# Turned memory probabilities in the raw-weight ring, and queries leaving PSUM by one engine after the other

## The chip, the cores and the metric

The kernel runs on one core of a Trainium2 chip. A time is the device time of one execution in microseconds (us), from the first to the last instruction and what little lies around it. The core has five engines with a queue each: TensorE (PE in the profile; its weight loads are PEld), VectorE (DVE), ScalarE (ACT), GpSimd (POOL) and SyncE (SP), which here only issues transfers. Each engine takes its instructions strictly in the order in which the program gives them, and waits at the head of its queue for the semaphores that the instruction needs. Matrix products land in PSUM, which has eight banks of 512 float32 per partition; VectorE and ScalarE read them from there.

## The reference

One inference step of a two-layer trunk, for a prompt of 512 tokens and a sample of 32 tokens, 544 columns in all. Layer 0 mixes tokens with RWKV-7, layer 1 with differential attention. Each layer is an RMS norm, one input projection, the token mixer, a cross-attention of four heads over 256 memory tokens, a SiLU gate, an output projection and a residual. The change touches layer 1 only:

```python
q, k, v, qm, gate = jnp.split(h @ w_in, [MIX_W, 2 * MIX_W, 3 * MIX_W, 3 * MIX_W + MEM_W], axis=-1)
...
attn = probs(q1, k1) - lam * probs(q2, k2)                  # 12 heads, two score maps each
o = rmsnorm(einsum('bhqk,bkhd->bqhd', attn, v_all), subln) * (1.0 - lam_init)
...
s = jnp.einsum('bthd,bmhd->bhtm', q, mk) * MEM_HD ** -0.5   # 4 memory heads of 128, 256 memory tokens
p = jax.nn.softmax(s, axis=-1)
y_mem = jnp.einsum('bhtm,bmhd->bthd', p, mv)
```

Outputs are the two token streams, the RWKV states and the keys and values of attention and memory.

## The kernel before, in words

**Layout.** Activations lie transposed: 128 features on the partitions, 544 tokens along the free axis. A projection is done in blocks of 128 output columns. One block is 48 matmuls: two halves of 272 tokens (one PSUM bank each, from the pool `psg` of three banks), and per half 8 slices of the 1024 inputs times 3 products (high part of the weight by high and low part of the activation, low part by high part). The loop is `steps`, line 463; one turn of it issues one matmul and is called a step below.

**Layer 1** (`diff_layer`, line 1940) is one stream of 56 such blocks: for each of the 12 heads a value, a key and a query block, then the gate blocks, and for heads 1, 3, 5 and 7 also a memory-query block and its gate. Everything else (scores, softmax, turning, DMA) is a list of events `ev`, each with a step at which it is issued. `at(f + x, ...)` puts an event x steps behind the begin f of its head. So the order of all queues is written out by hand: `Queue` and `tie` (lines 127 to 155) chain every instruction of an engine behind the one before it.

**Weights.** Layer 1's input projection uses scaled float16 weights. Their raw float32 blocks lie in four buffers in the space of the old low part of the activations (`h16s` in the profile). ScalarE writes the high half (`whs`), GpSimd scales the raw block and subtracts to get the low half. The power-of-two scale of a block is made by VectorE (`scales`, line 347) at step 36 of a block, from a sum that TensorE puts into column 480 of the bank that the block's first half uses. The earlier ring `raw` (pool `wp`, five buffers of 128 x 512 float32, line 1935) holds raw float32 halves in layer 0 and again for the output projection of layer 1. `self.ahead` is the list of blocks that are still to be loaded; its last 16 are those of the output projection.

**Queries.** `make_q` (line 1975) writes `qp`, the query split into a high part and a remainder for two row halves of 64 (the two score maps). For each half of the tokens, `parts` runs four instructions on one PSUM bank: ScalarE copies rows 0 to 63, VectorE subtracts that copy from the same rows; then the same for rows 64 to 127. In the second token half a ScalarE copy of the 32 sample columns (`qs`) follows. The framework lets no two engines touch one PSUM bank at a time, so of two instructions on one bank on different engines the later one in the program waits for the earlier.

**Memory heads in layer 1.** `mem_steps` (line 1217) is a generator with its turns at the steps of `MEMAT1`. The normalised probabilities of five token tiles are turned by VectorE in three pieces (two of 128 x 512, one of 128 x 256), at steps 330, 402 and 420 behind the begin f of the head (330, 400 and 430 for head 7). Each piece goes through `spread` (line 1911): VectorE transposes 32 x 32 blocks into the tile `to`, then SP stores `to` to DRAM in four parts (one part for the short piece), and a later load brings the turned matrix back (`mpT`). `to` has one buffer, so a turn waits until the stores of the turn before have landed. `spread` is called 15 times: 3 turns for each of 4 memory heads, and one for the cached keys of each of 3 groups of heads (4 steps behind the begin of heads 1, 5 and 9).

**Scores.** For each head, four tiles of scores (`scores`, `powers`, `turned`): TensorE writes two maps into the pools `psx` (one bank) and `psc` (two banks), VectorE takes the peaks (`snm`), ScalarE the exponentials (`pt`, `ps_s`), and VectorE joins and turns them (`pk`). TensorE's next tile of scores needs the bank of `psx`, which ScalarE's first exponential frees.

**The end.** The output projection (`w_out`, line 1346) loads its weights through the `raw` ring, and SP's queue also carries 12 copies of keys and values from DRAM to DRAM (`kv_out`, line 2239).

Of the kernel before, what the change touches and what calls it, by code (L numbers as in the profile page):

```python
# [9 lines left out]
F32 = mybir.dt.float32  # L10
# [4 lines left out]
AF = mybir.ActivationFunctionType  # L15
ALU = mybir.AluOpType
AX = mybir.AxisListType

P = 128
# [43 lines left out]
RAWS = 5  # L63
# [71 lines left out]
class Trunk:  # L135
# [1775 lines left out]
    def spread(self, x, rows, scr=None, blocks=range(4)):  # L1911

        if scr is None:
            scr = self.dp.tile([rows, P], F32, tag="spread", name="spread", bufs=4)[:]
        to = self.stage.tile([P, 512], F32, tag="to", name="to", bufs=1)[:, :rows]
        self.ve.transpose(to, x)

        def store():
            for b in blocks:
                self.se.dma_start(scr.rearrange("(n r) q -> r n q", r=32)[:, :, 32 * b : 32 * b + 32],  # L1920
                                  to[32 * b : 32 * b + 32].rearrange("p (n c) -> p n c", c=32))
            return scr

        return store
# [15 lines left out]
    def diff_layer(self, dq, p, mp, mctx, pool_early, order, made):  # L1940
# [6 lines left out]
        rows = [slice(0, 64), slice(64, P)]  # L1947
# [28 lines left out]
        def make_q(st):  # L1976
            def make(w):
                st["qp"] = qp = dq.tile([P, 2, T], F32R, tag="qp", name="qp", bufs=QB)

                def parts(ps, c):  # L1980
                    for m in range(2):
                        hi, inv = qp[rows[m], m, c], w[2][rows[m]]
                        self.ae.activation(hi, ps[rows[m], :], AF.Copy, scale=inv)
                        self.ve.scalar_tensor_tensor(qp[rows[1 - m], m, c], ps[rows[m], :], inv, hi.bitcast(F32),
                                                       ALU.mult, ALU.subtract)
                    if c.start:
                        self.ae.activation(st["G"]["qs"][:, st["j"], :], ps[:, TH - TS :], AF.Copy, scale=w[2])
                yield from self.steps(w, parts)
            return make

# [259 lines left out]
        for h, st in enumerate(sts):  # L2250
# [24 lines left out]
            if h in MEM1:  # L2275
                m = MEM1.index(h)
# [144 lines left out]
```

## Time and profile before

| what | value |
|---|---|
| median of 3 runs | 1396.15 us (1393.91 to 1396.59) |
| the profiled execution | 1400.69 us, of which the span is 1398.9 us |
| TensorE busy | 1315.5 us, 94% of the span |
| VectorE, ScalarE, GpSimd busy | 66%, 62%, 45% |
| granted TensorE clock, mean over the span | 0.981 of full |
| layer 1's input projection and attention | about 843 to 1262 us from the span's start |

How to read the profile's rows: a row of a timeline has the start (us from the span's start), the duration of the merged instructions, the engine, the line, the operation, `out<-in` by tile names, the shapes, and in square brackets the idle time of the engine just before and what ended it. Nearly all rows have line 132, that of the helper `Queue` that issues everything; the tile names tell them apart. A matmul's duration includes its latency, so rows of matmuls overlap. SPq rows are the issuing of transfers by SyncE.

### The profile page before, as it was taken

What the parts mean: (1) busy time and instruction counts of PE and PEld (TensorE: products, weight loads), DVE (VectorE), ACT (ScalarE), POOL (GpSimd) and SP (SyncE); (2) the same over time, 40 slices, a digit from 0 to 9 for tenths busy, and PEclk for the clock granted to TensorE, in tenths of its full rate; (3) what the DMA queues carried; (4) which work ended last, traced back from release to release, by engine and by line L of the source; (5) the groups of instructions that cost most, each with busy time, mean ns of one, the idle gap of its engine ahead of it and who ended that gap; (6) DMA issues with size and microseconds to landing.
All of it is one profiled execution on the core that took longest, in us unless ns stands there. A gap on an engine that the chain in (4) does not pass through costs nothing. (4 is left out here: it accounts for less than half of the span.)

```text
span 1398.9 us, 32065 instructions
## 1 busy us (share of the span) xinstructions
PE 1315.5 (94%) x11713; PEld 1195.5 (85%) x11713; DVE 925.5 (66%) x2391; ACT 862.9 (62%) x2316; POOL 624.5 (45%) x1103
## 2 busy tenths in 40 slices
PE   6999999999999999899999999989999998999797
PEld 6998899999999998898899987868777776878797
DVE  7766777787778777765763455656785568666343
ACT  7665677767776777565553367757655775773221
POOL 2227576556755585520120066545554554561000
PEclk9999999999999999999999999999999999999898
DMA  7542223332233323234384456766776667666421
GB/s 238 177 138 66 60 55 90 84 76 71 70 85 76 81 63 79 73 88 126 91 266 134 122 147 162 156 149 157 171 165 145 151 140 178 140 156 206 136 69 64
DMA packets 418296, 171.53 MB, mean 123 GB/s; under 512 B 195209, under 2 KB 402578, under 8 KB 418138
## 3 DMA queue, kind: packets, MB, share of 16 engines
q1 hardware_dynamic: 417994, 168.96, 46.3%
q8 instruction: 92, 1.51, 0.5%
q14 instruction: 66, 0.54, 0.1%
q10 hardware_dynamic: 144, 0.52, 0.1%
HBM read 130.84 MB, written 41.92 MB: 123 GB/s over the span
## 5 line engine op out<-in xcount | busy, mean ns | idle before, releaser
L132 PE MATMUL ps_g<-h,whs 128*128 128x272 f16 x2688 | 339.8, 282 | 15.2 <-POOL whs L132 11.8
L132 PEld LDWEIGHTS <-whs 128*128 128x128 f16 x2688 | 256.2, 99 | 73.3 <-POOL whs L132 15.7
L132 PE MATMUL ps_g<-hl,whi 128*128 128x272 f32 x976 | 284.2, 297 | 0.6 <-POOL hl L583 0.5
L132 PE MATMUL ps_g<-hh,wlo 128*128 128x272 f32 x912 | 277.8, 305 | 1.2 <-DVE wlo L132 1.2
L132 PE MATMUL ps_g<-hh,whi 128*128 128x272 f32 x912 | 275.0, 302 | 0.6 <-ACT hh L132 0.6
L872 POOL TENSOR_TENSOR tm<-u,m 102x84 f32<-102x84 f32 (+23 forms) x372 | 156.0, 419 | 165.9 <-DMA m<-sc 137.9
L132 DVE TENSOR_TENSOR wlo<-raw,whi 128x512 fp32r<-128x512 f32 x208 | 150.0, 736 | 84.5 <-ACT whi L132 80.9
L132 PEld LDWEIGHTS ps_g<-hl,whi 128*128 128x128 f32 x976 | 183.9, 191 | 2.4 <-POOL hl L583 0.7
L132 ACT CAST whi<-raw 128x512 fp32r<-128x512 f32 x210 | 125.3, 616 | 97.4 <-PE ps_g L132 45.4
L132 PEld LDWEIGHTS ps_g<-hh,whi 128*128 128x128 f32 x912 | 174.8, 192 | 4.1 <-ACT hh L132 1.0
L132 PEld LDWEIGHTS ps_g<-hh,wlo 128*128 128x128 f32 x912 | 174.2, 191 | 4.6 <-DVE wlo L132 1.9
L874 POOL TENSOR_TENSOR u<-u,tm 102x84 f32<-102x84 f32 (+23 forms) x372 | 159.5, 429 | 29.1
L132 POOL TENSOR_SCALAR h16s<-h16s 128x512 f32<-128x512 f32 x112 | 79.1, 717 | 151.5 <-ACT whs L132 150.3
L132 PE MATMUL ps_g<-hi,whi 128*128 128x272 f32 x448 | 130.6, 292 | 10.2 <-ACT hi L132 10.2
L132 PE MATMUL ps_g<-lo,whi 128*128 128x272 f32 x448 | 130.9, 292 | 1.2 <-DVE lo L132 1.1
L132 PE MATMUL ps_g<-hi,wlo 128*128 128x272 f32 x448 | 130.4, 291 | 0.5 <-DVE wlo L132 0.5
L132 POOL TENSOR_TENSOR whs<-h16s,whs 128x512 f16<-128x512 f32 x112 | 128.2, 1165 | 0.2
L132 PEld LDWEIGHTS ps_g<-hi,whi 128*128 128x128 f32 x448 | 85.5, 191 | 10.5 <-ACT hi L132 10.4
L132 PEld LDWEIGHTS ps_g<-lo,whi 128*128 128x128 f32 x448 | 85.5, 191 | 2.3 <-DVE lo L132 2.3
L132 PEld LDWEIGHTS ps_g<-hi,wlo 128*128 128x128 f32 x448 | 85.6, 191 | 0.9 <-DVE wlo L132 0.9
L132 DVE SCALAR_TENSOR_TENSOR SB<-ps_c,dl,sd 64x64 f32<-64x64 f32 x168 | 47.4, 282 | 42.9 <-PE ps_c L132 38.8
L132 ACT ACTIVATE whs<-h16s 128x512 f16<-128x512 f32 x112 | 74.9, 715 | 0.9 <-PE ps_g L132 0.9
(419 smaller groups left out, 2840.5 us busy)
## 6 DMA issues: line engine op xcount, KB each, us to landing
raw<-in_rw_in_dram SPq DMA_DIRECT2D x114, 256.0 KB
h16s<-in_df_in_dram SPq DMA_DIRECT2D x112, 256.0 KB
raw<-in_w_out_dram SPq DMA_DIRECT2D x64, 256.0 KB
ptr<-pk SPq DMA_DIRECT2D x44, 160.0 KB
aT<-ptr SPq DMA_DIRECT2D x11, 640.0 KB
scr<-sg SPq DMA_DIRECT2D x96, 68.0 KB
out_dram<-scr SPq DMA_DIRECT2D x6, 1024.0 KB
m<-sc SPq DMA_DIRECT2D x36, 128.0 KB
```

Of the source, the lines that this page charges most:

```text
L132: return lambda *a, **k: self.trunk.tie(self, issue(*a, **k))
L872: nc.gpsimd.tensor_tensor(tm[:, :n, :wd], u3[:, :n, kx : kx + 1].to_broadcast(sh), m3[:, kx : kx + 1, kx + 1 :].to_broadcast(sh), ALU.mult)
L874: nc.gpsimd.tensor_tensor(u3[:, :n, kx + 1 :], u3[:, :n, kx + 1 :], tm[:, :n, :wd], ALU.add)
```

## The change

Two edits. In `spread`, while more than 17 blocks are still to be loaded, the tile `to` is taken from the five buffers of the ring `raw` instead of its own single buffer. In `make_q`, ScalarE's copies of both row halves (and `qs`) come before VectorE's two subtractions in the program. No instruction, shape or transfer is added or taken away, and the order on each single engine is as before.

```diff
         if scr is None:
             scr = self.dp.tile([rows, P], F32, tag="spread", name="spread", bufs=4)[:]
-        to = self.stage.tile([P, 512], F32, tag="to", name="to", bufs=1)[:, :rows]
+        if len(self.ahead) > 17:
+            to = self.wp.tile([P, 512], F32, tag="raw", name="to", bufs=RAWS)[:, :rows]
+        else:
+            to = self.stage.tile([P, 512], F32, tag="to", name="to", bufs=1)[:, :rows]
         self.ve.transpose(to, x)
...
                 def parts(ps, c):
                     for m in range(2):
-                        hi, inv = qp[rows[m], m, c], w[2][rows[m]]
-                        self.ae.activation(hi, ps[rows[m], :], AF.Copy, scale=inv)
-                        self.ve.scalar_tensor_tensor(qp[rows[1 - m], m, c], ps[rows[m], :], inv, hi.bitcast(F32),
-                                                       ALU.mult, ALU.subtract)
+                        self.ae.activation(qp[rows[m], m, c], ps[rows[m], :], AF.Copy, scale=w[2][rows[m]])
                     if c.start:
                         self.ae.activation(st["G"]["qs"][:, st["j"], :], ps[:, TH - TS :], AF.Copy, scale=w[2])
+                    for m in range(2):
+                        self.ve.scalar_tensor_tensor(qp[rows[1 - m], m, c], ps[rows[m], :], w[2][rows[m]],
+                                                       qp[rows[m], m, c].bitcast(F32), ALU.mult, ALU.subtract)
                 yield from self.steps(w, parts)
```

## The prediction, made before the changed kernel was run

> **What bounds the kernel now.** I read the busy time by stretches first, then who waits for whom inside the stretch that the change touches, then the timelines of four engines around the longest waits. Stretches (columns: length; busy us and count of PE, PEld, DVE, ACT, POOL; granted clock; DMA share; GB/s):
>
> ```profile
> core 0 of [0], span 1398.9 us
> 843.00:1262.00 419.00, 389.35 (x3307) 319.21 (x3305) 277.52 (x826) 282.24 (x765) 228.68 (x238) 0.98 0.68 155
> ```
>
> The change lies in these 419 us. TensorE is busy for 389.35 of them, VectorE and ScalarE for about two thirds. So TensorE sets the pace there, and only its 29.65 us without work, and its time at a lower clock, can be won. TensorE's waits inside the stretch, and in layer 1 VectorE's and ScalarE's waits on the edited places (total, times, longest):
>
> ```profile
> PE ps_g L132 <- POOL whs L132: 10.3, 10, 2.3
> PE ps_s L132 <- ACT pt L132: 8.7, 5, 2.5
> PE ps_g L132 <- DVE h16s L132: 3.2, 2, 1.7
> PE ps_s L132 <- DVE os L132: 2.3, 1, 2.3
> ...
> DVE to L132 <- DMA mspread<-to: 17.8, 4, 7.2
> ...
> ACT qp L132 <- DVE qp L132: 45.6, 24, 8.1
> ```
>
> VectorE stands 17.8 us in front of the single tile `to`, four times, once per memory head. ScalarE stands 45.6 us in the 24 evacuations of queries, at the second row half each time. Neither engine is the bound, so what counts is which of these waits reach TensorE. Place A, in time order per engine (SP; DVE; ACT; PE):
>
> ```profile
> 916.74 5.13 SPq L132 DMA_DIRECT2D mspread<-to  x5
> ...
> 912.39 0.49 DVE L132 SCALAR_TENSOR_TENSOR qp<-ps_g,h16s,qp 64x272 fp32r<-64x272 f32 x1 [2.47 <-ACT qp L132]
> 913.44 0.51 DVE L132 SCALAR_TENSOR_TENSOR qp<-ps_g,h16s,qp 64x272 fp32r<-64x272 f32 x1 [0.55 <-ACT qp L132]
> 921.10 0.45 DVE L132 STREAM_TRANSPOSE to<-mp 128x256 f32<-128x256 f32 x1 [7.16 <-DMA mspread<-to]
> ...
> 924.87 0.49 DVE L132 TENSOR_REDUCE snm<-ps_s 128x1 f32<-128x128 f32 x2
> ...
> 922.73 0.48 ACT L132 ACTIVATE qp<-ps_g,h16s 64x272 fp32r<-64x272 f32 x1 [8.07 <-DVE qp L132]
> ...
> 926.33 0.35 ACT L132 ACTIVATE pt<-ps_s,snm 128x128 f32<-128x128 f32 x1
> ...
> 921.79 2.49 PE L132 MATMUL ps_g<-h,whs 128*128 128x272 f16 x20 [1.68 <-DVE h16s L132]
> 926.82 0.58 PE L132 MATMUL ps_s<-kh,qp 128*128 128x256 f32 x1 [2.54 <-ACT pt L132]
> ```
>
> The third turn of the memory head (921.10) waits 7.16 us until the stores of the second have landed; SP gets to them only at 916.74. Behind it in VectorE's queue stand the scales of a weight block and the first subtraction of the second query half. TensorE waits 1.68 us for the scales (they read column 480 of a bank that it needs). ScalarE waits 8.07 us for the subtraction, so its exponentials start late, and TensorE waits 2.54 us more for the bank of the next scores. One stall, two waits of TensorE.
>
> Such a wait costs a second time through the clock. Four stretches of 8 us:
>
> ```profile
> 924.00:932.00 8.00, 5.46 (x35) 4.06 (x33) 5.83 (x22) 6.43 (x20) 3.69 (x5) 0.79 0.59 169
> 1084.00:1092.00 8.00, 6.02 (x39) 4.55 (x40) 5.68 (x21) 6.39 (x20) 4.48 (x6) 0.79 0.51 144
> 1150.00:1158.00 8.00, 7.03 (x46) 5.42 (x47) 6.68 (x22) 4.41 (x14) 3.59 (x4) 0.79 1.01 264
> 1186.00:1194.00 8.00, 6.36 (x36) 4.21 (x35) 3.82 (x12) 4.92 (x14) 3.58 (x4) 0.79 0.92 213
> ```
>
> Each has a granted clock of 0.79: 8 x 0.21 = 1.68 us lost, the same each time, behind a wait of TensorE.
>
> **The change, part by part.** *The ring.* No instruction and no transfer is added; SP's order and VectorE's order stay. What changes is the buffer.
>
> ```profile
> L132 SPq DMA_DIRECT2D raw<-in_w_out_dram x14: 368/583/1987, 1240.1 to 1298.9; - x14
> L132 SPq DMA_DIRECT2D raw<-in_w_mem_v_dram x8: 367/376/1129, 800.7 to 814.9; - x8
> ```
>
> Between 814.9 and 1240.1 no load uses the ring (columns: duration min/median/max in ns, first and last start), so its five buffers are free for all turns; 15 turns also leave the ring at the same buffer for the output projection's loads. The condition holds for all: of 56 blocks and 16 of the output projection, 43 lie before head 9, where the last turn is, and at most 5 more are begun or loaded, which leaves 24 or more, above 17. Cost: nothing on any engine. The third turn then starts when the second subtraction ends, 913.44 + 0.51 = 913.95 instead of 921.10. The scales come about 1 us later, long before TensorE wants them (921.79 - 1.68 = 920.11). Between the turn's start and the peaks lie 924.87 - 921.10 = 3.8 us of VectorE's work, so the peaks of the first scores come at about 917.7 or, held by TensorE's own scores, a little later. Exponentials start 926.33 - 924.87 = 1.5 us behind them, near 920; TensorE wants the bank at 926.82 - 2.54 - 1.68 = 922.6. Both waits go, with some 2 us to spare, and with them the slow clock: 1.68 + 2.54 + 1.68 = **5.90 us**. SP no longer stands on the third store, so the weight loads behind it go out earlier, not later.
>
> *The queries.* Per token half the chain on one bank was copy 0.48, subtraction 0.49, copy, subtraction 0.51, with a gap of 0.55 on VectorE (913.44) in which the second copy runs. Now two copies, in second halves also the small `qs`, then two subtractions. Where both engines come in time, VectorE's gap of 0.55 goes but its first subtraction starts one copy later: 0.48 - 0.55 = 0.07 us earlier at the end, and in 12 second halves up to 0.48 later for `qs` (taken as no longer than the wider copy), so 0.41 late. Over 24 halves that is -1.7 to +4.9 us on VectorE's queue, whose next instructions (scales, `to`, peaks) have room; I take 0. Where VectorE comes late, it saves the full 0.55, and ScalarE never stands behind it: the 45.6 us go, and with them the delay of the exponentials and of the high halves of the weights queued behind.
>
> Where this reaches TensorE, by the remaining rows, in time order:
>
> ```profile
> 1080.95 2.49 PE L132 MATMUL ps_g<-h,whs 128*128 128x272 f16 x20 [1.52 <-DVE h16s L132]
> 1085.98 0.38 PE L132 MATMUL ps_s<-kh,qp 128*128 128x256 f32 x1 [2.54 <-ACT pt L132]
> ...
> 1004.57 0.39 PE L132 MATMUL ps_s<-kh,qp 128*128 128x256 f32 x1 [1.71 <-ACT pt L132]
> ...
> 1150.92 0.30 PE L132 MATMUL ps_s<-kh,qp 128*128 128x128 f32 x1 [2.31 <-DVE os L132]
> ...
> 1169.12 0.50 PE L132 MATMUL ps_s<-kh,qp 128*128 128x512 f32 x1 [0.68 <-ACT pt L132]
> 1179.92 0.63 PE L132 MATMUL ps_oT<-ident,ot 128*128 128x128 f32 x4 [1.60 <-DVE ot L132]
> 1188.75 0.63 PE L132 MATMUL ps_mo<-mpT,cmv 128*128 128x32 f32 x4 [1.64 <-DVE og L132]
> ...
> 1218.31 0.38 PE L132 MATMUL ps_s<-kh,qp 128*128 128x256 f32 x1 [1.27 <-ACT pt L132]
> ...
> 1162.36 0.45 DVE L132 STREAM_TRANSPOSE to<-mp 128x256 f32<-128x256 f32 x1 [2.61 <-DMA mspread<-to]
> ...
> 1214.74 0.48 ACT L132 ACTIVATE qp<-ps_g,h16s 64x272 fp32r<-64x272 f32 x1 [2.38 <-DVE qp L132]
> ```
>
> - B (1081 to 1092) repeats A: 1.52 + 2.54 + 1.68 = **5.74**.
> - C (1004.57): the same wait for an exponential, behind a VectorE that is late for both reasons: **1.71**.
> - D (1150.92): the scores wait for subtractions at a late VectorE, which saves two gaps of 0.55: **1.10** of 2.31.
> - E (1169.12): the fourth wait for `to`, 2.61 us, delays the exponentials: **0.68**.
> - F (1218.31): ScalarE lost 2.38 us at the query copy; TensorE's wait is shorter: **1.27**.
>
> Together 5.90 + 5.74 + 1.71 + 1.10 + 0.68 + 1.27 = **16.40 us**. Two terms have open size. Followers: the waits at 1179.92 and 1188.75 are for VectorE, which works without a pause after the late `to` of 1162.36 and gains two more gaps of 0.55, and the slow clocks at 1150 and 1186 stand behind shortened waits. Bounds 0 and 1.60 + 1.64 + 2 x 1.68 = 6.60; between ends with nothing nearer I take the middle, **3.30**. New waits: with these gone, GpSimd's low halves are the commonest wait, 10.3 / 10 = 1.03 us each. Bounds 0 and one more per head, 12.4; nothing puts more work on GpSimd, so I take two, **-2.06**. Sum: 17.6 us. The profiled execution took 1400.69 us (span 1398.9 and 1.8 around it), 4.5 above the median, so it would come to 1383.1; against the median 1396.15 - 17.6 = **1378.5 us**.
>
> The tail does not eat it:
>
> ```profile
> 1271.13 1.29 DVE wlo L132 x2
> ...
> 1277.06 14.14 DMA out_dram<-scr
> 1291.27 10.02 DMA raw<-in_w_out_dram
> ```
>
> These are rows of the chain that ended last. SP reaches the copies (14.14 us) only when VectorE's split of the ring's weights (1271.13) has freed the buffers of the loads before them, and that split follows TensorE's blocks. The whole tail moves with the stage.
>
> [...]
>
> **The rivals.**
>
> *Clock falls stay in number.* At A and B they re-form at other waits, at D and 1186 they stay, and no follower comes: 16.40 - 2 x 1.68 - 2.06 = 11.0, **1385.2 us**. For: 2.31 us of waiting was enough for a fall at 1150, and D keeps half of it. Against: A and B have no wait left. [...]
>
> *GpSimd takes over.* Its low halves become late once in every head: 12.4 instead of 2.06, gain 7.3, **1388.9 us**. For: it already has ten of TensorE's waits. Against: ScalarE's freedom starts it earlier.
>
> *Nothing arrives.* The stage ends earlier and the 14.14 and 10.02 us of transfers end at the same time: **1396.2**. Against: their start hangs on VectorE's split, above.
>
> *It doesn't do what it says.* If `to` stayed in its single buffer, A and B would keep their first wait, and D and F are left, 1.10 + 1.27: **1393.8**. Against: the count of blocks.
>
> *Slower.* VectorE's work that moves forward at the queries falls beside GpSimd's:
>
> ```profile
> 1180.36 0.67 DVE L132 TENSOR_TENSOR ot<-ot,oss 128x512 f32<-128x512 f32 x1
> ...
> 1182.64 1.65 DVE L132 TENSOR_TENSOR ot<-ot,oss 128x512 f32<-128x512 f32 x1
> ...
> L132 DVE SCALAR_TENSOR_TENSOR qp<-ps_g,h16s,qp x48: 493/500/507, 843.8 to 1237.8; 64x272 fp32r<-64x272 f32 x48
> ```
>
> The same product took 0.67 and 1.65, a price of 0.98. If the subtractions were stretched so and TensorE felt it, it decides from 17.6 / 0.98 = 18 of the 48; with 24 the time is 1396.15 - 17.6 + 23.5 = **1402.1 us**. Against: all 48 last 493 to 507 ns today, beside GpSimd or not.
>
> **How the numbers follow.** Forecast 0.52, clock 0.20, GpSimd 0.12, nothing 0.09, not done 0.03, slower 0.04. The likeliest alone reaches from 16.40 + 6.60 = 23.0 (1373.1) to 16.40 - 2.06 = 14.3 (1381.8). For 8 in 10 the range goes below it by 2 us and up past the clock and GpSimd cases: 1371 to 1391. A measurement of this kernel tells about 0.2% (2.8 us) from no change. Faster by more: 0.52 + 0.20 + 0.12 and half of "not done", 0.86; within: 0.09 and the rest, 0.10; slower 0.04.
>
> **What would show it.** Right: no wait of VectorE on `to` at all; ScalarE's waits for `qp` gone and VectorE's gaps of 0.55 gone; no wait of TensorE for the scales or, at A, B, C and F, for `pt`; granted clock 1.00 behind A and B. Wrong: `to` still waits; TensorE's waits for `whs` rise from 10.3 us towards 20; four or more stretches at clock 0.79; subtractions longer than 0.51; or a wait for the loads of the output projection that grows by what the stage gained.

## The result, and the profile after

The changed kernel takes 1376.33 us (median of 4 runs, 1373.41 to 1378.13) against 1395.95 for the kernel before in the same series: a ratio of 0.986, 95% interval 0.984 to 0.988, or 19.6 us less. Two later series gave 0.9861 (0.9839 to 0.9882) and 0.9868 (0.9847 to 0.9889). The forecast was 1378.5, with 1371 to 1391 as its range. The profiled execution took 1375.76 us (span 1374.0), 0.6 below its median.

The stretch of layer 1, 843 to 1242 us (same columns as before), and TensorE's waits from 843 to 1240 us:

```profile
843.00:1242.00 399.00, 385.26 (x3343) 320.83 (x3341) 279.57 (x835) 288.95 (x773) 232.40 (x240) 1.00 0.72 163
```

```profile
PE ps_g L132 <- POOL whs L132: 11.1, 10, 2.3
PE ps_s L132 <- DMA kh<-kh: 2.0, 1, 2.0
```

TensorE now lacks work for 13.7 us instead of 29.65, and the granted clock is 1.00 instead of 0.98. All its waits for the scales (`h16s`) and for the exponentials (`pt`) are gone; the ten for GpSimd's low halves are still ten. VectorE has no wait on `to`, and ScalarE none on VectorE for `qp`, where it stood for 45.6 us. The remaining waits at the queries are VectorE's:

```profile
DVE qp L132 <- ACT qp L132: 26.4, 9, 3.6
```

Place A, by the timelines of SP, VectorE, ScalarE and TensorE of the changed kernel:

```profile
917.23 2.81 SPq L132 DMA_DIRECT2D mspread<-to  x5
...
913.13 1.03 DVE L132 SCALAR_TENSOR_TENSOR qp<-ps_g,h16s,qp 64x272 fp32r<-64x272 f32 x2 [2.96 <-ACT qp L132]
914.19 0.45 DVE L132 STREAM_TRANSPOSE to<-mp 128x256 f32<-128x256 f32 x1
...
919.00 0.42 DVE L132 TENSOR_REDUCE snm<-ps_s 128x1 f32<-128x128 f32 x2
...
912.13 0.96 ACT L132 ACTIVATE qp<-ps_g,h16s 64x272 fp32r<-64x272 f32 x2
...
919.94 0.35 ACT L132 ACTIVATE pt<-ps_s,snm 128x128 f32<-128x128 f32 x1
...
919.72 2.94 PE L132 MATMUL ps_g<-h,whs 128*128 128x272 f16 x24
922.41 0.37 PE L132 MATMUL ps_s<-kh,qp 128*128 128x256 f32 x1
```

SP still gets to the stores only at 917.23, but the third turn no longer waits for them: it runs at 914.19. ScalarE's two copies follow each other without a gap (0.96 for two) and VectorE's two subtractions too (1.03). The exponential starts at 919.94, 2.47 us before TensorE wants the bank at 922.41, and neither of TensorE's rows has a wait.

Where the time went is read at the first scores of the heads, a point that TensorE itself sets. For heads 0, 3, 7 and 11, in the kernel before and then in the changed one:

```profile
847.12 0.31 PE L132 MATMUL ps_s<-kh,qp 128*128 128x128 f32 x1
...
952.35 0.31 PE L132 MATMUL ps_s<-kh,qp 128*128 128x128 f32 x1
...
1111.56 0.31 PE L132 MATMUL ps_s<-kh,qp 128*128 128x128 f32 x1
...
1237.22 0.30 PE L132 MATMUL ps_s<-kh,qp 128*128 128x128 f32 x1
```

```profile
848.06 0.31 PE L132 MATMUL ps_s<-kh,qp 128*128 128x128 f32 x1
...
946.31 0.31 PE L132 MATMUL ps_s<-kh,qp 128*128 128x128 f32 x1
...
1096.16 0.31 PE L132 MATMUL ps_s<-kh,qp 128*128 128x128 f32 x1
...
1214.37 0.30 PE L132 MATMUL ps_s<-kh,qp 128*128 128x128 f32 x1
```

| stretch (places in it) | before | after | gained | forecast |
|---|---|---|---|---|
| heads 0 to 3 (A) | 105.23 | 98.25 | 6.98 | 5.90 |
| heads 3 to 7 (C, B) | 159.21 | 149.85 | 9.36 | 7.45 |
| heads 7 to 11 (D, E, F, followers, new waits) | 125.66 | 118.21 | 7.45 | 4.29 |
| sum | 390.10 | 366.31 | 23.79 | 17.64 |

The tail moved with the stage. In the chains that ended last, VectorE's `wlo` stood at 1271.13 before; after, its timeline has it at 1247.52, and the chain ends with

```profile
1256.59 16.38 DMA out_dram<-scr
1273.03 4.97 DMA raw<-in_w_out_dram
```

together 21.4 us against 24.2 before. Nothing was given back there.

### The profile page after: what moved, and what is told of

Same layout as the page of the kernel before. It is cut to its first block, busy times and chain, and to the rows that moved or that the text cites. A ratio compares the mean times of both kernels' runs of the same rounds, so it can differ in the third digit from the quotient of the medians.

```text
span 1374.0 us, 32094 instructions
## 1 busy us (share of the span) xinstructions
PE 1304.3 (95%) x11713; PEld 1191.3 (87%) x11713; DVE 923.5 (67%) x2391; ACT 865.0 (63%) x2316; POOL 626.0 (46%) x1103
## 5 line engine op out<-in xcount | busy, mean ns | idle before, releaser
L132 PE MATMUL ps_g<-h,whs 128*128 128x272 f16 x2688 | 334.8, 280 | 12.5 <-POOL whs L132 12.5
```

What stands on the lines that cost most here:

```text
L132: return lambda *a, **k: self.trunk.tie(self, issue(*a, **k))
```

## The experiments

Kernels of one series share the runs of the kernel before. "The changed kernel" means both edits.

**Each edit alone, and both.** `e1_ring_only` has only the hunk in `spread`, `e2_query_only` only the hunk in `make_q`, `e3_both` is the changed kernel again.

> Only the first edit: the turned tile comes from the five-buffer ring, the query evacuation is as before. Theory T (one stall of VectorE in front of the single tile makes two waits of TensorE and a slow clock): VectorE's 17.8 us of waiting for the tile go to 0; TensorE's waits at A and B (1.68 + 2.54, 1.52 + 2.54) and two slow stretches of 1.68 go, also the 0.68 at E and half of the 1.71 at C; D (2.31) and F (1.27) stay. Sum 5.90 + 5.74 + 0.68 + 0.85 = 13.2 us, ratio to the kernel before 0.9906. Rival Q (the interleaved query evacuation is the cause, the tile only one of the things that make VectorE late): only the two waits for the scales go, 1.68 + 1.52 = 3.2 us, ratio 0.9977.

> Only the second edit: ScalarE's copies of both row halves ahead of VectorE's subtractions, the tile with its single buffer. Theory T: the waits for the scales at A and B stay (1.68 and 1.52), the waits for the exponentials shrink by about one half (VectorE's peaks are still late), D gives 1.1, F 1.27, C about 0.85: some 5 to 6 us, with the slow stretch at A or B perhaps staying; ratio 0.9960 (0.9945 to 0.9980). Rival Q: both waits of 2.54, C, D, F and the slow stretches go, 2 x (2.54 + 1.68) + 1.71 + 1.10 + 1.27 = 12.5 us, ratio 0.9910. If the edits were independent, the two gains would add up to that of both.

> The changed kernel again, on the chip and in the rounds of the other runs of this call, as their measure. Expected 0.986 (0.984 to 0.988) of the kernel before.

Measured: ring alone 1382.23 us, 0.9908 (0.9889 to 0.9927); queries alone 1386.71, 0.9938 (0.9920 to 0.9956); both 1375.51, 0.9861 (0.9839 to 0.9882); before 1395.18. In us: 12.95, 8.47, and 19.67 for both. The ring alone does what theory T said; the query order alone does somewhat more (8.5 us, its interval reaching into T's range), and the ratios of the rival (Q: 0.9977 and 0.9910) lie outside both intervals. The sum of the two is 1.75 above both together, too little for these intervals to tell from none; the rows show the overlap. TensorE's waits, 843 to 1255 us, ring alone and then queries alone:

```profile
PE ps_g L132 <- POOL whs L132: 11.2, 10, 2.3
PE ps_s L132 <- ACT pt L132: 1.9, 2, 1.3
```

```profile
PE ps_g L132 <- POOL whs L132: 9.9, 10, 2.3
PE ps_s L132 <- ACT pt L132: 3.4, 4, 1.5
PE ps_g L132 <- DVE h16s L132: 3.0, 2, 2.0
```

The ring takes away the waits for the scales; the query order alone leaves both of them (3.0 us) and still takes 5.3 of the 8.7 us of waits for exponentials. At A, queries alone:

```profile
920.04 3.80 PE L132 MATMUL ps_g<-h,whs 128*128 128x272 f16 x20 [2.02 <-DVE h16s L132]
924.08 0.55 PE L132 MATMUL ps_s<-kh,qp 128*128 128x256 f32 x1 [0.24 <-ACT pt L132]
```

VectorE still waits 7.51 us for `to`, but ScalarE does not stand behind its subtraction, and the second of TensorE's two waits shrinks from 2.54 to 0.24. So that wait had two causes in series, the late turn and ScalarE's place behind the subtraction, and at A either edit removes nearly all of it. There the gains overlap.

**The same wait, taken away without the ring.** On the kernel before, the third turn of heads 1, 3 and 5 comes 40 steps later, so that the stores of the second have landed, and the load of the turned matrix 16 later.

```diff
-MEMAT1 = (60, 80, 180, 276, 294, 306, 324, 330, 346, 362, 402, 420, 484, 552)
+MEMAT1 = (60, 80, 180, 276, 294, 306, 324, 330, 346, 362, 402, 460, 500, 552)
```

> The kernel before, with the single buffer and the interleaved queries as they were; for memory heads 1, 3 and 5 the third turn comes 40 steps later (460 instead of 420 behind the begin of the head, some 5 us of TensorE's blocks) and the load of the turned matrix 16 steps later (500 instead of 484). By then the stores of the second turn have landed and the query subtractions are past. Theory T (it is the wait's place in VectorE's queue that costs): VectorE's wait for the tile falls from 17.8 us to that of head 7, 2.6, and a remnant; A and B win 5.9 and 5.7 and C about 0.9, some 12 us, ratio to the kernel before 0.9915 (0.990 to 0.994), close to the first edit alone without any further buffer. Rival M (the wait only moves: at the new place the peaks and joins of the scores stand behind it): no gain, ratio 0.998 to 1.000, and TensorE waits for exponentials as before.

Measured: 1384.65 us, 0.9927 (0.9900 to 0.9954). VectorE's wait on `to` falls from 17.8 to 3.4 us (two times), TensorE's waits for the scales leave, and the time falls by 0.7% with neither the ring nor the query order, inside theory T's range; rival M falls. So the buffer is not the point; the wait of VectorE's whole queue at `to` is. Not issuing the turn so early took 8.95 us off the median of its series, where the ring took 12.95 off that of another.

**GpSimd's remaining waits.** On the changed kernel, the subtraction that makes the keys' remainder goes to VectorE, for both row halves (`e4_kz_dve`) or for one of them (`e6_kz_split`, repeated as `e9_kz_split_again` beside `e10_both_again`, the changed kernel).

```diff
-                self.ge.tensor_tensor(self.kz[h % 2][rows[m], m, :], k[rows[m], :], hi.bitcast(F32), ALU.subtract)
+                (self.ge if m else self.ve).tensor_tensor(self.kz[h % 2][rows[m], m, :], k[rows[m], :], hi.bitcast(F32), ALU.subtract)
```

> The changed kernel, and the two subtractions that make the low part of the keys (kz, 64 x 544 each) on VectorE instead of GpSimd. All of TensorE's waits of 0.8 to 2.3 us that are left in the stage are for GpSimd's low halves of the weights, 11.1 us in ten, and each stands behind the 2.75 us that GpSimd spends on kz. Theory P (kz on GpSimd is what is late now): these waits go, 8 to 11 us less than the changed kernel, ratio to the kernel before 0.979. Rival V: VectorE's queue takes 12 x 2 x 0.75 = 18 us more in front of the query subtractions, and the scores wait for it instead: no gain, or up to 5 us slower than the changed kernel (0.986 to 0.990).

> The changed kernel, with one of the two subtractions for the low part of the keys on VectorE and the other on GpSimd. Both on VectorE took TensorE's waits for GpSimd from 11.1 to 1.8 us, and as many waits for transfers and VectorE came in their place, without a gain. Theory L (TensorE is held by several queues that are late by about the same, transfers among them): half the load gives no gain either, 0.986 +- 0.002, with waits for GpSimd near 3 us and waits for the transfers of keys and of turned probabilities of about 4 us. Rival B (VectorE was overloaded by taking both): the split keeps VectorE in time, 5 us less than the changed kernel, ratio 0.9825.

> The changed kernel with one of the two subtractions of the keys' second half on VectorE and one on GpSimd, once more, beside the changed kernel on the same chip. Theory L (the split takes weight off GpSimd's queue and the waits for the low halves `whs` shrink from about 11 us to about 5, which reaches the end in part): 2 to 4 us below the changed kernel, ratio to before 0.983 to 0.985. Rival N (the first run's 2.5 us were scatter between calls): within 1 us of the changed kernel, both 0.985 to 0.987.

> The changed kernel as it is, beside the run with the subtraction split. Theory L: ratio to before 0.986, 2 to 4 us above the split one. Rival N: the two within 1 us. [...]

Measured: both on VectorE 1375.65 us, 0.9859 (0.9838 to 0.9881), no gain. Split 1372.99, 0.9845 (0.9818 to 0.9871), and again 1373.04, 0.9827 (0.9802 to 0.9852), where the changed kernel had 1377.68, 0.9868 (0.9847 to 0.9889). TensorE's largest waits, both on VectorE and then split:

```profile
PE ps_s L132 <- DMA kh<-kh: 3.4, 3, 2.5
PE ps_o L132 <- DMA aT<-ptr: 2.4, 4, 1.1
PE ps_mo L132 <- DVE og L132: 1.8, 2, 1.1
PE ps_g L132 <- POOL whs L132: 1.8, 2, 1.3
```

```profile
PE ps_g L132 <- POOL whs L132: 5.3, 8, 2.3
PE ps_s L132 <- DMA kh<-kh: 2.0, 2, 1.7
```

With both, the wait for `whs` falls from 11.1 to 1.8 us, and waits for VectorE and for transfers take its place: theory P falls, and the "no gain" of rival V came. With one, half of the wait goes and little comes. The first run of the split lies between what its own expectation gave (L, no gain; B, 5 us), with a longer wait for `whs` than L said (5.3 us for about 3) and a shorter one for transfers (2.0 for about 4). Its repetition had another L and a rival N, scatter. Side by side the split version is there 4.6 us ahead of the changed kernel; the intervals overlap a little (to 0.9852 and from 0.9847). Against versions of the changed kernel that differ only by the moves described next, it is 2.4 us ahead in each of two other series (1372.99 against 1375.34, 1372.81 against 1375.20). So the second L holds in kind (the wait for `whs` halves, to 4.7 us), and its 2 to 4 us are about what the three comparisons gave. By its medians, 1372.8 to 1373.0 in three series, the split is the fastest kernel found here.

**Place D.** The prediction read the wait of 2.31 us there as one for VectorE's subtractions. On the changed kernel, the keys' halves are sent at step 101 instead of 108 (`e7_keys_early`); then, beside that, the first turn of head 7's probabilities goes from step 330 to 342, so that SP meets `kh<-kh` ahead of that turn's stores (`e11_keys_first`; `e12_split_keys_first` is the same on the split version).

```diff
-MEMAT1B = MEMAT1[:10] + (400, 430, 490, 590)
+MEMAT1B = MEMAT1[:7] + (342, 346, 362, 400, 430, 490, 590)
...
-            for off, fn in ((52, values_turn), (62, lambda st: st["vout"]()), (99, keys), (108, keys_out)):
+            for off, fn in ((52, values_turn), (62, lambda st: st["vout"]()), (99, keys), (101, keys_out)):
```

> The changed kernel, with the transfers that copy the high part of the keys to the other row half (kh to kh, two per head) issued 7 steps earlier, at 101 instead of 108 behind the begin of the head; nothing else moves. At D the scores waited 2.31 us before the change and 1.99 us after it. Theory K (D was never VectorE: the scores wait for this transfer, which SP issues late behind the stores of turned probabilities and the first reads of the sample's values): the wait at D goes or falls below 0.7 us and with it the slow clock behind it, 2 to 4 us less than the changed kernel, ratio to the kernel before 0.984. Rival W (D is VectorE's late subtractions, as the prediction had it): D keeps its 2 us, ratio 0.986.

> The changed kernel with the halves of the keys sent 7 steps earlier and the first memory turn of head 7 put 12 steps later, so that at place D SP issues `kh<-kh` before the stores `mspread<-to` and no longer behind them. In six profiles TensorE's scores at D start 3.6 to 4.0 us after SP begins to issue `kh<-kh`, whatever VectorE does. Theory K (the wait at D is for that transfer): SP issues it about 2.3 us earlier, the 2.0 us wait goes or shrinks below 1.0, and the stretch at clock 0.79 behind it with it: 2 to 3.7 us below the changed kernel, ratio to before 0.983 to 0.985. Rival S (the wait is for VectorE's subtractions, as the prediction had it): SP's order is changed, the wait stays 1.7 to 2.3 us; ratio 0.986 to 0.987.

> The same two moves on the version whose key subtraction is split between VectorE and GpSimd (0.9827 and 0.9845 of before in its two measurements). Theory K: both gains add, ratio 0.979 to 0.982. Rival S: as without the moves, 0.983 to 0.985.

Measured: 1375.34 us, 0.9858 (0.9829 to 0.9888), for the earlier step alone; with the turn moved 1375.20, 0.9852 (0.9823 to 0.9881); split with both moves 1372.81, 0.9843 (0.9816 to 0.9870). SP and TensorE at D, changed kernel, then keys first:

```profile
1122.71 4.69 SPq L132 DMA_DIRECT2D ptr<-pk  x4
1127.44 1.22 SPq L132 DMA_DIRECT2D vs<-scr  x1
1128.76 2.20 SPq L132 DMA_DIRECT2D mspread<-to  x4
...
1131.67 1.11 SPq L132 DMA_DIRECT2D kh<-kh  x2
...
1135.63 0.30 PE L132 MATMUL ps_s<-kh,qp 128*128 128x128 f32 x1 [1.99 <-DMA kh<-kh]
```

```profile
1130.40 1.10 SPq L132 DMA_DIRECT2D kh<-kh  x2
...
1134.03 2.39 SPq L132 DMA_DIRECT2D mspread<-to  x4
...
1134.24 1.01 DVE L132 SCALAR_TENSOR_TENSOR qp<-ps_g,h16s,qp 64x272 fp32r<-64x272 f32 x2
...
1134.75 0.30 PE L132 MATMUL ps_s<-kh,qp 128*128 128x128 f32 x1
...
1143.56 1.60 PE L132 MATMUL ps_o<-vt,aT 128*128 128x128 f32 x12 [2.40 <-DMA aT<-ptr]
```

With the earlier step alone SP's order stays as it was: `kh<-kh` is still behind the stores of the turn, and the wait is still 1.68 us. By its number that run fits rival W, but since the order did not change it cannot tell K from W. With the turn moved the order changes and the wait at D is gone. TensorE's scores start at 1134.75, while VectorE's second pair of subtractions runs until 1134.24 + 1.01 = 1135.25, so they do not need it: theory K of the expectation, not S. On the split version the same moves take the wait from 1.74 to 0.26 us. The fall of the clock at D is gone as well; in this profile one of 1.68 us stands at the wait for `whs` near 1021 instead. But the time hardly moves. Between the first scores of heads 7 and 9 the keys-first version needs 70.38 us, the changed kernel 71.09: 0.7 us won of the 1.99 + 1.68 expected. TensorE now waits 2.40 us for `aT<-ptr`, a transfer that SP issued at 1136.02 in the changed kernel and at 1137.01 here. It lands 6.5 us after that (1143.56); in the changed kernel TensorE came to it 7.5 us after, because it had already stood at D. The ratios cannot decide: 0.9852 has an interval over the ranges of both theories, and 0.9843 of the split version lies in that of S. The rows decide: the mechanism of K holds, and its price of 2 to 3.7 us does not.

**The kernel before, profiled again.**

> The kernel before once more, for a second profile of it. [...]

Measured: 1392.05 us, span 1390.3, 8.6 us less than the execution on which the prediction rested. Its stretches with a low clock:

```profile
920.00:928.00 8.00, 6.75 (x43) 4.96 (x44) 5.59 (x21) 5.26 (x15) 3.61 (x4) 0.79 0.37 103
...
1000.00:1008.00 8.00, 6.31 (x40) 4.92 (x41) 5.90 (x21) 6.68 (x22) 4.49 (x6) 0.79 0.63 176
...
1144.00:1152.00 8.00, 6.43 (x44) 5.28 (x45) 6.03 (x21) 4.44 (x15) 3.60 (x4) 0.79 1.00 252
```

Three falls, at A, C and D; the first execution had four, at A, B, D and near 1186. So the number of falls differs between two executions of one program. The waits differ in part too: at B they are the same to 0.1 us (1.53 and 2.55 us, here without a fall), yet at A TensorE waits 2.21 and 0.97 us where it waited 1.68 and 2.54, and the wait for `whs` that was 2.29 us at 1030.70 is 0.28. At D this profile names the transfer, where the first named VectorE's `os`:

```profile
1145.57 0.45 PE L132 MATMUL ps_s<-kh,qp 128*128 128x128 f32 x1 [2.73 <-DMA kh<-kh]
```

Its first scores of heads 0 and 11 lie 384.88 us apart against 390.10, so against it the changed kernel gains 384.88 - 366.31 = 18.6 us in this stage, where the first profile gives 23.8. The changed kernel's other two profiles have 368.19 and 368.06. The means, 387.49 of two and 367.52 of three, differ by 20.0 us, close to the 19.6 of the medians.

## Why the prediction was right, and where it was not

**The direction and the main path: right.** Two thirds of the sum stood on one stall that is paid twice by TensorE (scales, then exponentials) and a third time by the clock. All three went at A and B. The turn came at 914.19 where the prediction had 913.95, the exponential at 919.94 where it had "near 920". The late start of the exponentials was a product of both edits' causes, as the runs with one edit show.

**A and B: slightly under-sized.** Between the first scores of heads 2 and 3 the gain is 6.28 us for A's 5.90, between heads 6 and 7 it is 6.16 for B's 5.74. What the sum left out may be the weight load: in PEld's rows these waits are 1.98 and 2.84 us where PE's rows have 1.68 and 2.54, 0.3 more each. No run tests this by itself. The clock's part of these terms was not certain: in the second profile of the kernel before, B has the same two waits and no fall of the clock, and heads 6 to 7 take 32.62 us there instead of 34.23. That both places fell in the profile on which the sum was built was chance, at B at least.

**C: right, with a neighbour left out.** From head 4 to head 5 the gain is 2.60 us: C's 1.71, and a wait of 0.72 us at 1022.63 for `og`, which left with VectorE's lateness and was in no term.

**D: wrong in its cause.** The step "the scores wait for subtractions at a late VectorE, which saves two gaps of 0.55" is refuted: they wait for the transfer of the keys' halves, which SP issues behind ten other transfers. In the kernel before, the scores start 1150.92 - 1147.21 = 3.71 us after the issue of `kh<-kh` begins, in the changed kernel 1135.63 - 1131.67 = 3.96. The wait shrank by 0.3 us, not 1.10, and the clock still falls there:

```profile
1136.00:1144.00 8.00, 8.00 (x58) 6.33 (x58) 7.16 (x28) 3.90 (x13) 3.59 (x4) 0.79 1.04 275
```

The row of before named "DVE os", and the prediction followed it, though the scores do not read `os`. They read `kh`, and SP's row of its issue lies only 3.7 us earlier, in the kernel before:

```profile
1147.21 1.11 SPq L132 DMA_DIRECT2D kh<-kh  x2
```

**E, F and the followers: the middle was too low.** The waits at 1179.92 and 1188.75, with the fall at 1186, are gone, so of the bound of 6.60 all but the fall at D came (4.92), not 3.30. F is 1.27 and arrived: heads 10 to 11 gained 2.04, of which 0.50 is a shorter wait for `whs` (1.72 to 1.22).

**New waits: over-sized.** One wait for GpSimd grew, from 0.28 to 1.50 us, the same block in both (the kernel before, then two rows of the changed one):

```profile
1182.68 1.10 PE L132 MATMUL ps_g<-h,whs 128*128 128x272 f16 x8 [0.28 <-POOL whs L132]
...
1022.06 1.10 PE L132 MATMUL ps_g<-h,whs 128*128 128x272 f16 x8 [2.28 <-POOL whs L132]
...
1165.73 1.10 PE L132 MATMUL ps_g<-h,whs 128*128 128x272 f16 x8 [1.50 <-POOL whs L132]
```

With the shorter one at F the total rose by 0.8 us, not 2.06. The row at 1022.06 was there before at the same length (2.29 us at 1030.70).

**The price of the query edit on VectorE, taken as nothing: borne out.** In the view of the tile `qp`, the durations are unchanged:

```profile
L132 DVE SCALAR_TENSOR_TENSOR qp<-ps_g,h16s,qp x48: 493/500/507, 845.2 to 1214.4; 64x272 fp32r<-64x272 f32 x48
```

So no subtraction was stretched beside GpSimd (the two at 913.13 took 1.03 us beside its `h16s` and `whs` of 912.40 to 915.99), and the slower case had nothing to stand on.

**The base.** The errors of the terms add up to 6.2 us in the stage (23.8 against 17.6), yet the time was missed by only 2.2. The sum was set against the profiled execution and then moved to the median with its size unchanged. In the series of the result that execution lies 4.7 us above the median and the changed kernel's 0.6 below its own, so 5.3 of the profiles' 24.9 us are not in the medians. Against the second profile of before, the stage gains 18.6. The good agreement of 1378.5 with 1376.33 is therefore partly two deviations that cancel: a low sum, and a profile that showed more to win than an average execution has.

**The rivals.** "Nothing arrives" fell: VectorE's split at the end came 23.6 us earlier, and the last transfer of the chain ended 23.3 us earlier (1278.00 instead of 1301.29). "It doesn't do what it says" fell with the 45.6 and 17.8 us. "GpSimd takes over" is right in that the ten waits for `whs` are now TensorE's largest group, but they cost about what they did before (11.1 us for 10.3); taking half of them away, as the split does, was worth 2.4 to 4.6 us. "Clock falls stay in number" fell for this profile (four to one); how far a fall goes with its wait is seen in the next section but one.

## What to carry to other kernels

The single buffer of `to` was priced by everything behind it in VectorE's queue: VectorE waited 17.8 us for it, and the ring alone won 12.95 us of the time. With such a tile, follow the queue until the engine that sets the pace waits, and expect the same stall to appear there under other names. On a PSUM bank that two engines may not touch together, let one engine finish before the other begins; alternating here put ScalarE behind VectorE's whole queue, 45.6 us of waiting, and the query order alone won 8.47 us. Before a wait is ascribed to the engine that a row names, list what the waiting instruction reads, and look for a transfer that the issuing queue reaches late; when such a wait is removed, look at once at the next transfer in that queue.

## What the runs showed of the hardware that was not expected

**The same wait does not always slow the clock.** Three profiles of the changed kernel have the wait for `whs` near 1022 us with 2.3 us. In the first the clock stays at 1.00 behind it; in the one of `e10_both_again` it does not:

```profile
1021.57 1.93 PE L132 MATMUL ps_g<-h,whs 128*128 128x272 f16 x8 [2.29 <-POOL whs L132]
```

```profile
1016.00:1024.00 8.00, 5.71 (x41) 4.56 (x40) 7.27 (x17) 6.67 (x16) 7.72 (x8) 0.85 0.89 218
1024.00:1032.00 8.00, 8.00 (x68) 6.99 (x67) 5.25 (x21) 3.16 (x11) 2.33 (x3) 0.93 0.91 184
```

8 x (0.15 + 0.07) = 1.76 us are lost, one fall by the size of 1.68, and heads 4 to 7 show it: 105.53 us instead of 103.87. At 8 us a stretch the one fall lies across two. The falls in the stage were four and three in the two profiles of the kernel before, one, two and two in the three of the changed one. In ten of the profiles the wait is 2.28 or 2.29 us long. Behind it the four matmuls of `ps_oT` take 0.60 us in three of the ten (both kernels' first profiles and `e12_split_keys_first`) and 0.87 to 1.06 us in seven (`e1`, `e2`, `e3`, `e6`, `e9`, `e10`, `e11`). What decides between the two the traces do not show; they show that at 2.3 us the outcome differs from execution to execution. A term for the clock at such a wait of this kernel is thus a chance times 1.68 us, and not the count of falls in one profile.

**At D the wait for a transfer followed its place in the issuing queue.** In the changed kernel, ScalarE had written `kh` by 1126.61 (its row: 1125.30, 1.31 us), and SP, with 4.69, 1.22 and 2.20 us for the groups ahead of it, issued the transfer at 1131.67; TensorE waited 1.99 us. Issued at 1130.40, ahead of the stores, it left TensorE no wait. Removing the 1.99 us there moved the lateness to the next transfer, `aT<-ptr`, with 2.40 us.
